# Low parts of weight tiles: an accumulating DMA instead of a VectorE difference

## The chip, the cores and the metric

The kernel runs on 1 core of one Trainium2 chip. The metric is the device time of one execution in microseconds (us). The kernel before takes 1283.22 us, the median of 3 runs (1282.95 to 1283.3). About 0.2% is what a measurement of it can tell from no change.

## The reference

One encoder block for 512 tokens of width 1024, in float32. Two half feed-forwards stand around a token mixer:

```python
x = x + 0.5 * swiglu_ffn(rms_norm(x, ffn1_norm[l]), ffn1_w_gate[l], ffn1_w_up[l], ffn1_w_down[l])
h = rms_norm(x, mix_norm[l])
proj = h @ w_in[l] + b_in[l]
u_a, v_a, q_r, k_r, v_r, g_r, gate_a, gate_b = jnp.split(proj, split_at, axis=-1)
a = spatial_gating(gelu(u_a), gelu(v_a), ...)                    # 128-token chunks
r = bidirectional_retention(rotary(q), rotary(k) / 16, v, ...)   # 4 heads of 256
r = normalised(r) * silu(g_r)
mix = sigmoid(gate_a) * (a @ w_branch_a[l]) + sigmoid(gate_b) * (r @ w_branch_b[l])
x = x + mix @ w_out[l]
x = x + 0.5 * swiglu_ffn(rms_norm(x, ffn2_norm[l]), ffn2_w_gate[l], ffn2_w_up[l], ffn2_w_down[l])
return rms_norm(x, final_norm)
```

`swiglu_ffn(h)` is `(silu(h @ w_gate) * (h @ w_up)) @ w_down` with 2816 hidden units. Nearly all the work is the matrix products with the weights.

## The kernel before

A product in float32 is made of three TensorE passes. Each operand is split into a high part, the value rounded to the type `float32r`, and a low part, the value minus the high part. `mm3` (L90 to L93) adds high times high (L91), the activations' low times the weights' high (L92), and the activations' high times the weights' low (L93; in the token-major products the operands of L92 and L93 change places).

The weights come in tiles. `load_w` (L79) makes one: SP loads the raw tile from HBM by one DMA (L82), ScalarE casts it to the high part (L85), VectorE subtracts (L87). Raw, high and low tiles come from a pool `wp` with 2 buffers each; a buffer is free when its last reader is done. A tile is 128 x 2048 elements, 1,024 KB: 8 rows of blocks of 128 along K and 256 columns of the weight, in pieces of 1 KB in HBM (or 4 rows and 512 columns in the token-major products). TensorE does 48 matmuls with a tile.

There are 106 such tiles. The first feed-forward has 10 pairs of a gate and an up tile (`ag`, `au`; a first pair is loaded in pieces, apart) and 12 down tiles (`ad`, the last four of 768 KB). The mixer has 24 (`q`, `k`, `pv`, `g`, `pva`, `u`), the merge 16 (`ga`, `gb`, `wa`, `wb`), the output projection 4 (`wo`), the second feed-forward 11 pairs (`bg`, `bu`) and 8 down tiles (`bd`). Its last down chunk is split tile by tile elsewhere (`last_weights`).

In `ffn`, `gate_up` uses a pair of tiles in turns: for each half j of the columns first the gate tile, then the up tile. So the order on TensorE is gate j=0, up j=0, gate j=1, up j=1, and then the next pair. Down tiles and the mixer's tiles are used whole, one after the other. `down(0)` stands behind pair 4, `down(1)` behind pair 8.

The norm's factor is applied behind the products: `norm.stats` puts sums on TensorE behind the first gate half, a `pow` on Pool (L132) gives the inverse root, and `spread` brings it to all partitions by a product on TensorE. The loads of the first up tile of a feed-forward and of the first `k` tile are put behind the last square of the norm's sum (`norm.behind`).

The order on each engine is set by a scheduler at build time, from the program order and from the buffers that come free; each engine then runs its instructions in that order. Only the beginning (`first`, the first pair in whole tiles) and the end (`last`) are in written order. Pool does nearly nothing: some memsets, one iota and the `pow`s.

Of the kernel before, what the change touches and what calls it, by code (L numbers as in the profile page):

```python
# [9 lines left out]
F32 = mybir.dt.float32  # L10
# [5 lines left out]
P = 128  # L16
# [13 lines left out]
OFF_U, OFF_V, OFF_Q, OFF_K, OFF_VR, OFF_G, OFF_GA, OFF_GB = (i * 1024 for i in range(8))  # L30
# columns of the per-feature vectors
C_G1, C_GM, C_G2, C_GF, C_B = 0, 8, 16, 24, 32
C_N = 96
# row vectors, broadcast over the partitions
R_BV, R_BVR, R_SG, R_SB, R_BS, R_DEC = 0, 1024, 2048, 3072, 4096, 4608
# [4 lines left out]
def block_kernel(ctx, tc, xT, wg1, wu1, wd1, w_in, wa, wb, wo, wg2, wu2, wd2, cols_d, rows_d, ws_d, cos_d, sin_d, out):  # L40
    nc = tc.nc
    act = ctx.enter_context(tc.tile_pool(name="act", bufs=60))
    wp = ctx.enter_context(tc.tile_pool(name="wp", bufs=2))
    sc = ctx.enter_context(tc.tile_pool(name="sc", bufs=6))
    sm = ctx.enter_context(tc.tile_pool(name="sm", bufs=2))
# [12 lines left out]

# [1 line left out]
    cols = const.tile([P, C_N], F32, name="cols")  # L60
# [11 lines left out]
    def split(src, name, lo_pool=None):  # L72
        """The two parts of a float32 tile that one TensorE pass carries exactly."""
        hi = A(name + "_hi")
        nc.scalar.copy(hi, src)
        lo = A(name + "_lo") if lo_pool is None else lo_pool.tile([P, S], F32R, tag="lo", name=name + "_lo")
        nc.vector.tensor_tensor(out=lo, in0=src, in1=hi.bitcast(F32), op=ALU.subtract)
        return hi, lo

    def load_w(w, k0, nk, c0, nc_, name):  # L80
        raw = wp.tile([P, nk, nc_], F32, tag="raw", name=name + "_raw")
        nc.sync.dma_start(  # L82
            out=raw, in_=w[k0 * P:(k0 + nk) * P, c0:c0 + nc_].rearrange("(k p) c -> p k c", p=P))
        hi = wp.tile([P, nk, nc_], F32R, tag="whi", name=name + "_whi")
        nc.scalar.copy(hi, raw)  # L85
        lo = wp.tile([P, nk, nc_], F32R, tag="wlo", name=name + "_wlo")
        nc.vector.tensor_tensor(out=lo, in0=raw, in1=hi.bitcast(F32), op=ALU.subtract)  # L87
        return hi, lo
# [6 lines left out]
    def proj(o, wt, j, acts, first=True, last=True):  # L95
        """o[feature, token] += w[:, j-th 128 columns].T @ acts"""
        whi, wlo = wt
        n = len(acts)
        for k, (hi, lo) in enumerate(acts):
            mm3(o, whi[:, k, j * P:(j + 1) * P], wlo[:, k, j * P:(j + 1) * P], hi, lo,  # L100
                first and k == 0, last and k == n - 1)

    class Norm:
        """Sum of squares of feature-major tiles, and from it the inverse root mean square."""

# [10 lines left out]
        def behind(self):  # L116
            """Order what follows behind the last term of the sum."""
            stack = ExitStack()
            for ins in self.ins:
                stack.enter_context(tc.issue_after(ins))  # L120
            return stack

        def stats(self, n):
            """Per token, with tokens on the partitions; then on a diagonal, to be spread by `spread`."""
            pt = PS(self.name + "_pss")
# [21 lines left out]
        def spread(self):  # L147
            """The same along the free axis, on all partitions."""
            pb = PS(self.name + "_pbc")
            nc.tensor.matmul(pb, ones_r, self.diag[0], start=True, stop=False)  # L150
            nc.tensor.matmul(pb, ones_r, self.diag[1], start=False, stop=True)
            return pb
# [6 lines left out]
    def scaled_split(x, col, name):  # L159
        """Both parts of x * cols[:, col]."""  # L160
        g = cols[:, col:col + 1]
        hi = A(name + "_hi")
        nc.scalar.activation(hi, x, AF.Copy, scale=g)
        lo = A(name + "_lo")
        nc.vector.scalar_tensor_tensor(out=lo, in0=x, scalar=g, in1=hi.bitcast(F32), op0=ALU.mult, op1=ALU.subtract)
        return hi, lo

    started = []

# [1 line left out]
    def ffn(tag, x, h, norm, wg, wu, wd, on_x, first=None, last=None, last_weights=None, aside=None):  # L171
        """x += 0.5 * swiglu(h); h lacks the factor 1 / rms, which norm gives."""
        bc = None
# [81 lines left out]

# [1 line left out]
    x = [A(f"x{k}", F32) for k in range(KT)]  # L257
    h = []
    norm = Norm("n1")

    def first(pss):
        """The first weights come in pieces along K, so that TensorE can start on the first ones."""
        warm = T("warm")
# [36 lines left out]
    def tables():  # L300
        """Rotary and decay tables of the heads, and the biases of their values."""
        with tc.issue_after(started[0]), tc.issue_after(started[1]), tc.issue_after(started[2]):
# [5 lines left out]

            # log_sigmoid(z) = min(z, 0) - log1p(exp(-|z|)), log1p(e) = 2 atanh(e / (2 + e))
            lg = hp.tile([P, 8], F32, name="lg")  # L310
# [16 lines left out]

            # decay of query t and key s by u = t - (s - p): E[p, u + 384]
            dd = wp.tile([P, 2, EW], F32, tag="raw", name="dd")
# [12 lines left out]

# [1 line left out]
    def bias(col):  # L344
        return cols[:, C_B + col // P:C_B + col // P + 1]

    def tok_proj(o, wt, j0, nk, j, k0, first, last):
        """o[token, column] += h2.T @ w for one tile of tokens"""
        whi, wlo = wt
        for i in range(nk):  # L350
            k = k0 + i
            hi, lo = h2[k][0][:, j * P:(j + 1) * P], h2[k][1][:, j * P:(j + 1) * P]
            mm3(o, hi, lo, whi[:, i, :], wlo[:, i, :], first and i == 0, last and i == nk - 1)

    def tok_block(col, name, between=None):
        """Projection of 512 columns with tokens on the partitions."""
        pv = [PS(name) for _ in range(NT)]
        for half in range(2):
            wt = load_w(w_in, 4 * half, 4, col, 512, f"{name}{half}")
            for j in range(NT):  # L360
                tok_proj(pv[j], wt, 0, 4, j, 4 * half, half == 0, half == 1)
            if half == 0 and between is not None:
                between()
        return pv
# [122 lines left out]

# [1 line left out]
    with ExitStack() as sctx:  # L489
# [86 lines left out]

# [1 line left out]
    mix = []  # L578
# [43 lines left out]

# [1 line left out]
    lp = ctx.enter_context(tc.tile_pool(name="lp", bufs=6))  # L624
# [12 lines left out]
    def last(w, acts):  # L637
        """The last part of the down projection, the final norm and the output, by halves of the tokens,
        so that the first half's norm runs behind the second half's products."""
        nf = len(acts)  # L640
# [75 lines left out]
def _tables():  # L716
    """Rotary angles: they depend on the shapes alone."""
    d = 256
# [38 lines left out]
```

## Time and profile before

| | |
|---|---|
| median of 3 runs | 1283.22 us |
| profiled execution, span | 1281.6 us |
| TensorE busy | 1270.8 us (99%) |
| VectorE busy | 653.1 us (51%) |
| ScalarE busy | 393.6 us (31%) |
| Pool busy | 12.1 us (1%) |
| DMA, share of 16 engines | 30.9%, 126.94 MB |

The profiled execution's span runs from its first to its last instruction; the time of a run is 1.6 us more in the median. An engine's busy time is the sum of its instructions. Matmuls overlap, so a matmul's duration (0.39 us) is longer than the distance to the next (0.227 us); the distance is what counts. The chain that ended last tells which engine sets the end, and the waits of that engine tell what it lacked.

### The profile page before, as it was taken

To read this page: it belongs to the slowest core of one execution; us is meant where nothing else is said; L and a number is where in the kernel's file an instruction comes from. 1 tells how busy PE (TensorE), PEld (TensorE's weight loads), DVE (VectorE), ACT (ScalarE), POOL (GpSimd) and SP (SyncE) were. 2 spreads that over 40 slices of the span, in tenths; PEclk is the share of its full clock that TensorE was granted. 3 is DMA by queue.
4 is the path that set the end of the run, shared out by engine and by line. 5 is a ranking of instruction groups with operands and counts; after the bars stand their busy time and mean duration, and the time that the engine had idled before them with its cause. 6 is when DMAs were issued, how large, how long until landed. Compare 5 with 4: busy or idle time off the path is not lost.

```text
span 1281.6 us, 13501 instructions
## 1 busy us (share of the span) xinstructions
PE 1270.8 (99%) x5787; PEld 1056.0 (82%) x5787; DVE 653.1 (51%) x789; ACT 393.6 (31%) x427; POOL 12.1 (1%) x17
## 2 busy tenths in 40 slices
PE   9999999999999999999999999999999999999997
PEld 6888888888888888888888888888888888888897
DVE  6644355534467575675297434345544434353453
ACT  6322124212243232333244222223322212231232
POOL 0000000000000000000000000000000000000000
PEclk9999999999999999999999999999999999999998
DMA  8223313322343223234223333343242322233221
GB/s 283 80 66 131 98 58 108 111 91 87 113 158 99 66 66 99 67 99 131 66 66 99 99 99 99 99 152 112 66 131 66 129 90 91 86 102 96 90 75 66
DMA packets 116155, 127.79 MB, mean 100 GB/s; under 512 B 2944, under 2 KB 106368, under 8 KB 116096
## 3 DMA queue, kind: packets, MB, share of 16 engines
q1 hardware_dynamic: 116096, 126.94, 30.9%
q8 instruction: 45, 0.74, 0.2%
q14 instruction: 14, 0.11, 0.0%
HBM read 122.74 MB, written 4.19 MB: 99 GB/s over the span
## 4 chain that ended last, share of the span: by engine, by line
PE 99%; DMA 0%; DVE 0%; SPq 0%; ACT 0%; POOLq 0%; issue 0%; DVEq 0%; ACTq 0%
PE apg L91 3%; PE bpd L91 3%; PE bpd L93 3%; PE bpd L92 3%; PE apg L92 3%; PE apg L93 3%; PE apu L91 3%; PE apu L92 3%; PE apu L93 3%; PE bpu L91 3%; PE bpu L93 3%; PE bpg L93 3%; PE apd L92 3%; PE bpg L92 3%; PE apd L91 3%; PE bpu L92 3%
## 5 line engine op out<-in xcount | busy, mean ns | idle before, releaser
L91 PE MATMUL bpu<-h_hi,bu_whi 128*128 128x512 f32 x176 | 68.6, 390 | 0.0
L93 PE MATMUL bpu<-h_hi,bu_wlo 128*128 128x512 f32 x176 | 68.5, 389 | 0.0
L93 PE MATMUL bpg<-h_hi,bg_wlo 128*128 128x512 f32 x176 | 68.5, 389 | 0.0
L92 PE MATMUL bpg<-h_lo,bg_whi 128*128 128x512 f32 x176 | 68.5, 389 | 0.0
L91 PE MATMUL bpg<-h_hi,bg_whi 128*128 128x512 f32 x176 | 68.5, 389 | 0.0
L92 PE MATMUL bpu<-h_lo,bu_whi 128*128 128x512 f32 x176 | 68.5, 389 | 0.0
L91 PE MATMUL apd<-ahid_hi,ad_whi 128*128 128x512 f32 x176 | 68.5, 389 | 0.0
L92 PE MATMUL apd<-ahid_lo,ad_whi 128*128 128x512 f32 x176 | 68.5, 389 | 0.0
L93 PE MATMUL apd<-ahid_hi,ad_wlo 128*128 128x512 f32 x176 | 68.5, 389 | 0.0
L91 PE MATMUL apu<-h_hi,au_whi 128*128 128x512 f32 x160 | 62.4, 390 | 0.0
L93 PE MATMUL apu<-h_hi,au_wlo 128*128 128x512 f32 x160 | 62.3, 389 | 0.0
L93 PE MATMUL apg<-h_hi,ag_wlo 128*128 128x512 f32 x160 | 62.3, 389 | 0.0
L92 PE MATMUL apg<-h_lo,ag_whi 128*128 128x512 f32 x160 | 62.3, 389 | 0.0
L91 PE MATMUL apg<-h_hi,ag_whi 128*128 128x512 f32 x160 | 62.2, 389 | 0.0
L92 PE MATMUL apu<-h_lo,au_whi 128*128 128x512 f32 x160 | 62.2, 389 | 0.0
L91 PE MATMUL bpd<-bhid_hi,bd_whi 128*128 128x512 f32 x128 | 49.8, 389 | 0.0
L92 PE MATMUL bpd<-bhid_lo,bd_whi 128*128 128x512 f32 x128 | 49.8, 389 | 0.0
L93 PE MATMUL bpd<-bhid_hi,bd_wlo 128*128 128x512 f32 x128 | 49.8, 389 | 0.0
L222 DVE SCALAR_TENSOR_TENSOR x<-apd,x 128x512 f32<-128x512 f32 x24 | 16.6, 692 | 58.0 <-PE apd L93 58.0
L203 DVE TENSOR_TENSOR btu<-bpu,n_bc 128x512 f32<-128x512 f32 x22 | 15.2, 691 | 59.0 <-PE bpu L93 59.0
L203 DVE TENSOR_TENSOR atu<-apu,n_bc 128x512 f32<-128x512 f32 x22 | 15.2, 689 | 49.2 <-PE apu L93 49.2
L92 PEld LDWEIGHTS bpu<-h_lo,bu_whi 128*128 128x128 f32 x176 | 33.1, 188 | 6.9
(302 smaller groups left out, 3141.2 us busy)
## 6 DMA issues: line engine op xcount, KB each, us to landing
bg_raw<-in_wg SPq DMA_DIRECT2D x11, 1024.0 KB, 5.3
bu_raw<-in_wu SPq DMA_DIRECT2D x11, 1024.0 KB, 5.3
ag_raw<-in_wg SPq DMA_DIRECT2D x10, 1024.0 KB, 5.3
au_raw<-in_wu SPq DMA_DIRECT2D x10, 1024.0 KB, 5.5
ad_raw<-in_wd SPq DMA_DIRECT2D x8, 1024.0 KB, 5.1
bd_raw<-in_wd SPq DMA_DIRECT2D x8, 1024.0 KB, 5.0
q_raw<-in_w_in SPq DMA_DIRECT2D x4, 1024.0 KB, 5.4
k_raw<-in_w_in SPq DMA_DIRECT2D x4, 1024.0 KB, 5.3
```

Of the source, the lines that this page charges most:

```text
L91: nc.tensor.matmul(o, lhi, rhi, start=first, stop=False)
L92: nc.tensor.matmul(o, lhi, rlo, start=False, stop=False)
L93: nc.tensor.matmul(o, llo, rhi, start=False, stop=last)
L203: nc.vector.tensor_tensor(out=tut, in0=pu, in1=bc, op=ALU.mult)
L222: nc.vector.scalar_tensor_tensor(out=x[m], in0=pd[j], scalar=0.5, in1=x[m], op0=ALU.mult, op1=ALU.add)
```

## The change

The raw load and the cast stay. The low part is now made in two steps: ScalarE writes the raw tile times -1 into the low tile, whose type `float32r` rounds it, so that it holds minus the high part; then a DMA from Pool's queue reads the raw weights once more from HBM and adds them onto the tile. VectorE has no part in it. The raw tile's last reader is now on ScalarE. The low tiles get a pool of their own, `wl`, with 3 buffers instead of 2, and the pool of activation tiles gives up 3 of its 60 buffers for it. Comments and doc strings are dropped, which changes only line numbers.

```diff
-    act = ctx.enter_context(tc.tile_pool(name="act", bufs=60))
+    act = ctx.enter_context(tc.tile_pool(name="act", bufs=57))
     wp = ctx.enter_context(tc.tile_pool(name="wp", bufs=2))
+    wl = ctx.enter_context(tc.tile_pool(name="wl", bufs=3))
...
         hi = wp.tile([P, nk, nc_], F32R, tag="whi", name=name + "_whi")
         nc.scalar.copy(hi, raw)
-        lo = wp.tile([P, nk, nc_], F32R, tag="wlo", name=name + "_wlo")
-        nc.vector.tensor_tensor(out=lo, in0=raw, in1=hi.bitcast(F32), op=ALU.subtract)
+        lo = wl.tile([P, nk, nc_], F32R, tag="wlo", name=name + "_wlo")
+        nc.scalar.activation(lo, raw, AF.Copy, scale=-1.0)
+        nc.gpsimd.dma_start(out=lo, in_=w[k0 * P:(k0 + nk) * P, c0:c0 + nc_].rearrange("(k p) c -> p k c", p=P),
+                            accum_op=ALU.add)
         return hi, lo
```

The order of ScalarE's instructions between pairs 3 and 4 of the first feed-forward. `whi` is a cast, `wlo` a negated copy, `atg` a Silu of a gate half, `ahid_hi` the cast of a hidden unit. Before:

```order
L201 ACTIVATE atg_761<-atg_761 128x512
L75 CAST ahid_hi_767<-atu_764 128x512
L85 CAST ag4_whi_783<-ag4_raw_781 128x2048
L201 ACTIVATE atg_771<-atg_771 128x512
L85 CAST au4_whi_789<-au4_raw_787 128x2048
L75 CAST ahid_hi_777<-atu_774 128x512
```

The same stretch in the changed kernel:

```order
L88 ACTIVATE ag4_wlo_794<-ag4_raw_790 128x2048
L204 ACTIVATE atg_770<-atg_770 128x512
L76 CAST ahid_hi_776<-atu_773 128x512
L86 CAST ag4_whi_792<-ag4_raw_790 128x2048
L204 ACTIVATE atg_780<-atg_780 128x512
L88 ACTIVATE au4_wlo_801<-au4_raw_797 128x2048
L86 CAST au4_whi_799<-au4_raw_797 128x2048
```

The negated copy of the gate tile stands nearly a pair ahead of its cast; that of the up tile comes behind the cast of the gate tile and a Silu, and just ahead of its own cast.

The order on Pool around pairs 3 and 4 in the changed kernel; before there is nothing here but the `pow` (L132, now L135):

```order
L89 DMA ag2_wlo_526<-in_wg1 128x8x256
L135 TENSOR_TENSOR n1_tok_391<-n1_var_389,neghalf_88 128x4
L89 DMA au2_wlo_533<-in_wu1 128x8x256
L89 DMA ag3_wlo_660<-in_wg1 128x8x256
L89 DMA au3_wlo_667<-in_wu1 128x8x256
L89 DMA ag4_wlo_794<-in_wg1 128x8x256
L89 DMA au4_wlo_801<-in_wu1 128x8x256
```

Each accumulating DMA waits in this queue for its negated copy, and what stands behind it waits too.

ScalarE at the start of the second feed-forward, before, with the last square of the norm (`n3_sq`) and the first up tile:

```order
L163 ACTIVATE h3_hi_6046<-xb7_5764,cols_75 128x512
L111 ACTIVATE n3_sq_6050<-xb7_5764 128x512
L85 CAST bu0_whi_6064<-bu0_raw_6062 128x2048
L156 COPY n3_bc_6135<-n3_pbc_6136 128x512
L201 ACT_TABLE_LOAD
```

The same stretch in the changed kernel:

```order
L166 ACTIVATE h3_hi_6125<-xb7_5839,cols_78 128x512
L114 ACTIVATE n3_sq_6129<-xb7_5839 128x512
L86 CAST bu0_whi_6144<-bu0_raw_6142 128x2048
L88 ACTIVATE bu0_wlo_6146<-bu0_raw_6142 128x2048
L88 ACTIVATE bg1_wlo_6295<-bg1_raw_6291 128x2048
L159 COPY n3_bc_6216<-n3_pbc_6217 128x512
```

The cast still comes behind the last square, and the negated copy behind the cast. On TensorE at the same place the changed kernel has the product that spreads the norm (`n3_pbc`) ahead of the first use of `bu0_wlo`:

```order
L131 MATMUL n3_pss_6174<-ones_79,n3_sq_6129 128x2 x4
L94 MATMUL bpu_6191<-h3_hi_5874,bu0_whi_6144 128x512
L95 MATMUL bpu_6191<-h3_lo_5876,bu0_whi_6144 128x512
L153 MATMUL n3_pbc_6217<-n3_diag_hi_6187,ones_r_81 128x512
L154 MATMUL n3_pbc_6217<-n3_diag_lo_6189,ones_r_81 128x512
L96 MATMUL bpu_6191<-h3_hi_5874,bu0_wlo_6146 128x512
```

Before, that product stands behind the whole up half. The low part is still wanted by the third matmul of the up tile. Elsewhere on TensorE only the order within the scores of two heads differs.

## Rows read from the trace of the kernel before

**Rows 1.** The page: busy time by engine, and the chain that ended last.
```profile
span 1281.6 us, 13501 instructions
...
PE 1270.8 (99%) x5787; PEld 1056.0 (82%) x5787; DVE 653.1 (51%) x789; ACT 393.6 (31%) x427; POOL 12.1 (1%) x17
...
PE 99%; DMA 0%; DVE 0%; SPq 0%; ACT 0%; POOLq 0%; issue 0%; DVEq 0%; ACTq 0%
```
**Rows 2.** Waits of TensorE, all: us in total, times, longest.
```profile
PE n_pbc L693 <- DVE n_diag L687: 1.5, 1, 1.5
PE warm L269 <- DVE warm L264: 1.3, 1, 1.3
PE apg L91 <- ACT first_hi L75: 1.1, 1, 1.1
PE n_pss L680 <- ACT n_sq L667: 0.7, 1, 0.7
```
**Rows 3.** Groups by line and form: busy us, mean ns of one; idle before.
```profile
L85 ACT CAST bu_whi<-bu_raw 128x2048 fp32r<-128x2048 f32 x11 | 21.1, 1915 | 41.9 <-issue 24.0 <-PE bpd L92 17.9
...
L75 ACT CAST ahid_hi<-atu 128x512 fp32r<-128x512 f32 x22 | 13.5, 620 | 45.9 <-DVE atu L204 45.9
L163 ACT ACTIVATE h_hi<-x,cols 128x512 fp32r<-128x512 f32 x16 | 11.6, 725 | 20.8 <-DVE x L222 18.1 <-DMA cols<-in_cols 1.7 <-DMA x<-in_xT 0.8
...
L87 DVE TENSOR_TENSOR bu_wlo<-bu_raw,bu_whi 128x2048 fp32r<-128x2048 f32 x11 | 25.2, 2292 | 5.3 <-ACT bu_whi L85 5.3
```
**Rows 4.** The DMA view: one queue, then issues, KB each, median us to landing.
```profile
q1 hardware_dynamic: 116096, 126.94, 30.9%
...
bg_raw<-in_wg SPq DMA_DIRECT2D x11, 1024.0 KB, 5.3
...
ad_raw<-in_wd SPq DMA_DIRECT2D x8, 1024.0 KB, 5.1
...
ad_raw<-in_wd SPq DMA_DIRECT2D x4, 768.0 KB, 4.4
```
**Rows 5.** Timeline between pairs 3 and 4, ScalarE, then TensorE: start us, us.
```profile
91.67 1.91 ACT L85 CAST ag_whi<-ag_raw 128x2048 fp32r<-128x2048 f32 x1 [3.11 <-PE apg L92]
93.49 0.62 ACT L201 ACTIVATE atg<-atg 128x512 f32<-128x512 f32 x1
...
102.76 0.39 PE L92 MATMUL apu<-h_lo,au_whi 128*128 128x512 f32 x1
102.98 0.39 PE L93 MATMUL apu<-h_hi,au_wlo 128*128 128x512 f32 x1
```
**Rows 6.** Timeline between pairs 1 and 2, ScalarE and TensorE.
```profile
50.98 1.13 ACT L75 CAST ahid_hi<-atu 128x512 fp32r<-128x512 f32 x2
...
59.47 0.39 PE L93 MATMUL apu<-h_hi,au_wlo 128*128 128x512 f32 x1
```
**Rows 7.** Timeline of the start, ScalarE and TensorE.
```profile
21.32 1.91 ACT L85 CAST ag_whi<-ag_raw 128x2048 fp32r<-128x2048 f32 x1 [3.13 <-DMA ag_raw<-in_wg]
...
30.78 0.39 PE L93 MATMUL apg<-h_hi,ag_wlo 128*128 128x512 f32 x1
```
**Rows 8.** Timeline at head 0's key tile, ScalarE and TensorE.
```profile
371.17 1.90 ACT L85 CAST k_whi<-k_raw 128x2048 fp32r<-128x2048 f32 x1
...
381.88 0.40 PE L93 MATMUL k<-h_hi,k_wlo 128*128 128x512 f32 x1
```
**Rows 9.** Timeline at the second feed-forward's first up tile, ScalarE and TensorE.
```profile
908.69 1.89 ACT L85 CAST bu_whi<-bu_raw 128x2048 fp32r<-128x2048 f32 x1
...
913.42 0.40 PE L93 MATMUL bpu<-h_hi,bu_wlo 128*128 128x512 f32 x1
```
**Rows 10.** The end by stretches (PEclk after POOL busy), timelines of end and start.
```profile
1273.00:1282.00 9.00, 1.22 (x2) 0.50 (x2) 2.91 (x5) 0.00 (x0) 0.69 (x1) 0.53 0.34 117
...
1270.49 0.28 PE L680 MATMUL n_pss<-ones,n_acc 128*128 128x2 f32 x2
...
10.08 0.63 PE L93 MATMUL apg<-h_hi,first_lo 128*128 128x512 f32 x1
10.51 0.45 PE L91 MATMUL apu<-h_hi,first_hi 128*128 128x512 f32 x1
```

## The prediction

> **What bounds the kernel now.** I read the page's totals and the chain of work that ended last, then who waited for whom on TensorE, then the timeline around the places where a weight tile is first used. TensorE is busy 1270.8 us of the 1281.6 us span, and the chain is 99% TensorE [rows 1]. Its only waits are four, 1.5, 1.3, 1.1 and 0.7 us, and none is for a low part of a weight tile [rows 2]. So there is nothing behind the VectorE difference to win: VectorE is busy 653.1 us, half the span [rows 1], and a VectorE that does less moves no end. The question is only whether the new way delivers each low part before TensorE wants it. The profiled span is 1281.6 us; the median of the runs is 1283.2 us, so I add 1.6 us to a span.
>
> **What is removed.** 106 differences on VectorE (32 tiles in the first feed-forward, 24 in the mixer, 20 in the merge and the output projection, 30 in the second feed-forward), 102 of 2.29 us [rows 3]: some 240 us of work that lies beside TensorE. Gain on the path: 0. I exclude a gain, since no TensorE wait stands behind these instructions.
>
> **What is added on ScalarE.** 106 negated copies of a raw tile, same shape as the cast, 1.91 us [rows 3]. A scaled 128x512 takes 725 ns where a cast of that shape takes 620 [rows 3], so 2.3 us is the upper bound if the scale costs per element; it is a constant here, so I take 1.91. That is 106 x 1.91 = 202 us more on an engine busy 393.6 of 1281.6 us [rows 1]; it fits. What counts is where a copy stands in ScalarE's order (below).
>
> **What is added on the DMA queues.** 106 accumulating transfers on Pool's queue, of 1,024 KB (four of 768). None is in the trace. A plain load of 1,024 KB lands 5.3 us after its issue; 768 KB land in 4.4 us and 1,024 KB in 5.1 us for the same tensor [rows 4]. By these two, 256 KB cost 0.7 us, so a load is 2.3 us fixed and 2.8 us of data. An accumulating one reads the weights, reads what lies in the tile, and writes. Let X be the time from the end of the negated copy to the landing. Lower bound: a plain load, 5.3 us; I exclude less, because the same bytes come from HBM in the same 1 KB pieces. Upper bound: three passes in turn, 3 x 5.3 = 15.9 us, which leaves room for Pool's own part in the issue. I take 2.3 + 2 x 2.8 = 7.9 us for two reads, plus 2.8 us because SP starts the next raw load while it runs: X = 10.7 us.
>
> By the Trainium skill ("DMA: Bandwidth & Descriptors", Anatomy of one DMA — SWDGE (gpsimd) path) a Pool transfer takes 2.0 us plus its bytes at 436 GB/s: 4.4 us for this tile, as an estimate. The plain load from SP took 5.3 us here, longer than that, and no row shows a Pool transfer; with 4.4 us the sum below would be 3.5 us and the time 1286.7 us. The same skill ("Collectives: The Full Stack", The bandwidth ceiling) says that a reducing transfer has half the rate of a copy, for its two source reads. That speaks for doubling the data term, and against the change.
>
> **DMA capacity.** The 106 tiles are 107,520 KB = 110.1 MB of the 126.94 MB that take 30.9% of the DMA engines [rows 4], so 26.8% is theirs. At twice the cost the new transfers need 53.6%, in all 84.5%: it fits. At 2.6 times the sum reaches 100%.
>
> **How long each place can wait.** The low tiles now rotate through three buffers, so a copy can start when the tile three back is used up. Where tiles are used one after the other (down projections, mixer, merge), one tile of 48 matmuls lasts 10.9 us (0.22 to 0.23 us apart, [rows 5], 0.227 in the mean), and two lie between: over 18 us for X, hidden. It is different in the gate/up pairs, because a pair uses its two tiles in turns: gate, up, gate, up, 5.4 us each. The up tile of pair p+1 takes the buffer of the gate tile of pair p, which is free only after its second turn. In ScalarE's new order the high cast of the next gate tile and a Silu stand first, then the negated copy. In the trace that cast starts at 91.67 us and the Silu ends at 94.11 [rows 5], so the copy would end at 96.0. TensorE wants that low part at 102.98 [rows 5]: **room 7.0 us**, stall X - 7.0 = 3.7 us. This holds for pairs 3, 4, 6, 7, 8, 10 of the first and 1, 2, 3, 4, 6, 7, 8, 10 of the second feed-forward, where the pair follows a pair: 14 x 3.7 = **51.8 us**. A stall moves the next release by as much, so it comes again at each pair.
> - Pair 2 of the first feed-forward: two more hidden-unit casts stand before the copy. They end at 52.1 us [rows 6], the copy at 54.0, the low part is wanted at 59.47 [rows 6]: room 5.5, stall **5.2 us**.
> - The start: the first gate cast ends at 23.2 us [rows 7], the copy at 25.1, the wish is at 30.78 [rows 7]: room 5.7, stall **5.0 us**. The up tile's cast and copy follow until 28.9; its wish comes 24 matmuls after the gate tile's, past 36.2, so its room is 7.3 us plus the first stall, and it adds nothing.
> - Key tile of head 0, which is held back behind the norm's last square: cast from 371.17 us, copy until 375.0, wanted at 381.88 [rows 8]: room 6.9, stall **3.8 us**.
> - The first up tile of the second feed-forward, held back in the same way: cast from 908.69 us, copy until 912.5, wanted at 913.42 [rows 9]: room 0.9, stall **9.8 us**. Before, the 2.29 us difference ended just in time. This place stalls by 4.4 us even at the plain load's X. The norm's `pow` stands behind this transfer on Pool; TensorE needs it only 2 matmuls into the tile, and what it loses there lies inside the same stall, as long as the issue takes Pool under 9 us.
>
> Three activation buffers fewer, and a wo load that now stands ahead of one of the reloaded x tiles on SP: the x tile is wanted only after its first output projection, so I price both at 0; if that cover were gone it would be at most a full plain load, 5.3 us [rows 4].
>
> **Sum.** 51.8 + 5.2 + 5.0 + 3.8 + 9.8 = 75.6 us; 1281.6 + 75.6 + 1.6 = **1358.8 us**. At X = 5.3 only 913.42 stalls: 4.4 us, 1287.6 us. At X = 15.9: 14 x 8.9 + 10.4 + 10.2 + 9.0 + 15.0 = 169.2 us, 1452.4 us.
>
> **Rivals.**
> - *A fast transfer* (X from 3.5 to 7.0). The pairs hide it; left are 913.42 and little else: 1286 to 1296 us. For it: plain loads land in 5.3 us, and the engines are two thirds idle. Against: a second read, and Pool must make the issue. The Trainium skill's fit (above) would put the time here.
> - *The transfer becomes the bound* (X over 13.5, or more than 2.6 times a plain load on the engines). At three times, 30.9 + 3 x 26.8 = 111% of the span: 1426 us by capacity, 1452 us by latency, more if one issue keeps Pool for over 10.9 us a tile. For it: no row shows what the addition or Pool's issue costs.
> - *The clock falls in the stalls.* At the end TensorE does only 128x2 matmuls from 1270.49 us, waits 1.5 us [rows 2], and the granted clock of the last 9 us is 0.53, which is the 1.2 GHz level [rows 10]. At the start matmuls stand 0.43 us apart until 10.51 us and then at full pace [rows 10]. If every one of 18 stalls cost some 10 matmuls at 0.2 us more, that is 36 us: 1395 us.
> - *Not slower.* It decides at one place, 913.42: with X at 3.5 us or less the stall there is 2.6 us or less and all others are gone, so the time is at most 1285.8 us. It needs an accumulation that lands before a plain load would. Against: even 768 KB take 4.4 us plain [rows 4].
>
> **How the numbers follow.** Forecast (X 7 to 13.5, 1297 to 1410 us) 0.45; fast transfer 0.18; bound by transfers 0.22; clock 0.12; not slower 0.03. The range runs from the lower to the upper bound of X, 1288 to 1452 us, and leaves out the last case, the lowest part of the fast one and half of the bound one. About 0.2%, 2.6 us, is what a measurement can tell from no change: faster 0.01 and same 0.02 (the two together are the last case), slower 0.97.
>
> **What would show it.** In the profile after: waits of TensorE for the low tiles, by a DMA from Pool; about 3.7 us at each of 14 pairs, about 10 us at the first up tile of the second feed-forward, none in the down projections and the merge; the accumulating transfers landing some 10 us after their issue; VectorE near 410 us, ScalarE near 595; DMA share near 80%. Waits in the down projections too would mean the engines or Pool are the bound. If the pairs show no wait, X is under 7. A granted clock under 1.0 between pairs would show the clock rival. The prediction is wrong if ScalarE's copies start later than their place says, for then the rooms are shorter than I read them.

## Result and profile after

The changed kernel takes 1394.92 us (median; 1394.79 to 1395.37), the kernel before 1283.2 us (1282.95 to 1283.3): ratio 1.0874, 95% interval 1.0858 to 1.0889. It is slower by 112 us, where 75.6 us were forecast. In the fences below line numbers are three higher than in the rows of before (a high cast is L86, the negated copy L88, Pool's transfer L89, the three products L94 to L96).

The page of the changed kernel, first its span, then busy time by engine (us, share of the span, instructions) and the DMA queues (q0 is Pool's, q1 SP's: packets, MB, share of 16 engines):

```profile
span 1393.6 us, 13794 instructions
...
PE 1303.9 (94%) x5787; PEld 1074.3 (77%) x5787; DVE 421.9 (30%) x683; ACT 582.6 (42%) x535; POOL 175.5 (13%) x123
...
q0 software_dynamic: 105120, 110.11, 50.6%
q1 hardware_dynamic: 116096, 126.94, 28.3%
```

Against [rows 1]: VectorE gave up 231 us and nothing came of it; TensorE's share fell from 99% to 94%. Two things happened to TensorE. It **waits** 89.7 us (1393.6 - 1303.9) where it waited 10.8 (1281.6 - 1270.8): 78.9 us more. And its **busy time grew** by 33.1 us (1303.9 against 1270.8) for the same 5787 matmuls. Together 112.0 us, which is all of the difference of the spans.

The waits of TensorE in the changed kernel (us in total, times, longest), to be held against the four of [rows 2]:

```profile
PE bpu L96 <- DMA bu_wlo<-in_wu: 32.3, 9, 5.7
PE apu L96 <- DMA au_wlo<-in_wu: 26.9, 7, 6.1
PE apg L96 <- DMA ag_wlo<-in_wg: 8.8, 1, 8.8
PE k L96 <- DMA k_wlo<-in_w_in: 4.4, 1, 4.4
PE n_pbc L153 <- DVE n_diag_hi L143: 2.8, 1, 2.8
PE nr_pbc L153 <- DVE nr_diag_hi L143: 2.4, 1, 2.4
```

The four large ones are for a low part, by a DMA, at gate/up pairs, the start and the key tile of head 0; the last two, at products that spread a norm, come below. One pair in the timeline (start us, us), ScalarE, Pool, then TensorE; it answers to [rows 5]:

```profile
87.29 1.91 ACT L86 CAST ag_whi<-ag_raw 128x2048 fp32r<-128x2048 f32 x1 [3.12 <-PE apg L95]
89.11 0.63 ACT L204 ACTIVATE atg<-atg 128x512 f32<-128x512 f32 x1
89.63 1.90 ACT L88 ACTIVATE au_wlo<-au_raw 128x2048 fp32r<-128x2048 f32 x1
...
91.83 1.55 POOL L89 DMA_DIRECT2D au_wlo<-in_wu  x1 [22.08 <-ACT au_wlo L88]
...
101.64 0.50 PE L96 MATMUL apu<-h_hi,au_wlo 128*128 128x512 f32 x1 [2.88 <-DMA au_wlo<-in_wu]
```

Cast, Silu and negated copy stand in ScalarE's order as the forecast had them. The copy ends at 91.53 us, the low part is wanted at 98.76 (101.64 less the 2.88 of waiting) and is there at 101.64: the room, from the copy's end to the wish, is 7.2 us, and the time to the landing 10.1 us. Pool is free for 22 us before, so no queue on Pool holds this transfer up.

The extra busy time stands behind the waits. TensorE after another one, that of pair 2:

```profile
73.82 0.80 PE L96 MATMUL apu<-h_hi,au_wlo 128*128 128x512 f32 x1 [4.75 <-DMA au_wlo<-in_wu]
74.41 0.63 PE L94 MATMUL apu<-h_hi,au_whi 128*128 128x512 f32 x1
74.83 0.63 PE L95 MATMUL apu<-h_lo,au_whi 128*128 128x512 f32 x1
...
80.21 0.39 PE L96 MATMUL apu<-h_hi,au_wlo 128*128 128x512 f32 x1
80.44 0.39 PE L94 MATMUL apu<-h_hi,au_whi 128*128 128x512 f32 x1
```

For 6 us the matmuls start 0.43 us apart, then 0.23 again. The same by stretches (us, busy time of PE, PEld, DVE, ACT and POOL, then the granted clock, DMA share, GB/s):

```profile
74.00:80.00 6.00, 6.00 (x15) 4.70 (x16) 0.00 (x0) 0.00 (x0) 0.00 (x0) 0.50 1.18 204
...
480.00:560.00 80.00, 80.00 (x358) 66.27 (x358) 42.81 (x69) 37.57 (x38) 10.13 (x7) 1.00 0.78 166
720.00:960.00 240.00, 240.00 (x1093) 200.01 (x1092) 73.30 (x112) 111.99 (x94) 33.66 (x22) 1.00 0.94 198
```

The granted clock is 0.50, the 1.2 GHz level, behind the wait (the DMA share of so short a stretch is rough). In a stretch of the mixer (480 to 560 us) and from the mixer's end through the merge into the output projection (720 to 960 us) TensorE never waits, at a DMA share up to 0.94, and its clock stays at 1.00.

### The profile page after: what moved, and what is told of

Same layout as the page of the kernel before. It is cut to its first block, busy times and chain, and to the rows that moved or that the text cites. A ratio compares the mean times of both kernels' runs of the same rounds, so it can differ in the third digit from the quotient of the medians.

```text
span 1393.6 us, 13794 instructions
## 1 busy us (share of the span) xinstructions
PE 1303.9 (94%) x5787; PEld 1074.3 (77%) x5787; DVE 421.9 (30%) x683; ACT 582.6 (42%) x535; POOL 175.5 (13%) x123
## 3 DMA queue, kind: packets, MB, share of 16 engines
q0 software_dynamic: 105120, 110.11, 50.6%
## 4 chain that ended last, share of the span: by engine, by line
PE 47%; issue 36%; DMA 8%; POOL 5%; ACT 3%; DVE 1%; SPq 0%; POOLq 0%; DVEq 0%; ACTq 0%
DMA u_raw<-in_w_in 2%; DMA bu_wlo<-in_wu 2%; PE pgt L94 2%; PE pgt L96 2%; PE pgt L95 2%; PE bpd L94 2%; PE bpd L95 2%; PE bpd L96 2%; PE k L96 1%; PE k L94 1%; PE k L95 1%; PE po L96 1%; PE pb L96 1%; PE pb L94 1%; PE pa L96 1%
## 5 line engine op out<-in xcount | busy, mean ns | idle before, releaser
L96 PE MATMUL bpu<-h_hi,bu_wlo 128*128 128x512 f32 x176 | 75.2, 427 | 32.3 <-DMA bu_wlo<-in_wu 32.3
L96 PE MATMUL apu<-h_hi,au_wlo 128*128 128x512 f32 x160 | 68.1, 426 | 26.9 <-DMA au_wlo<-in_wu 26.9
L94 PE MATMUL bpu<-h_hi,bu_whi 128*128 128x512 f32 x176 | 73.3, 417 | 0.0
L95 PE MATMUL bpu<-h_lo,bu_whi 128*128 128x512 f32 x176 | 73.3, 416 | 0.0
L96 PE MATMUL apg<-h_hi,ag_wlo 128*128 128x512 f32 x160 | 63.4, 396 | 8.8 <-DMA ag_wlo<-in_wg 8.8
L96 PEld LDWEIGHTS bpu<-h_hi,bu_wlo 128*128 128x128 f32 x176 | 36.1, 205 | 44.0 <-DMA bu_wlo<-in_wu 36.2
L94 PE MATMUL apd<-ahid_hi,ad_whi 128*128 128x512 f32 x176 | 68.5, 389 | 0.0
L96 PE MATMUL apd<-ahid_hi,ad_wlo 128*128 128x512 f32 x176 | 68.5, 389 | 0.0
L94 PE MATMUL bpg<-h_hi,bg_whi 128*128 128x512 f32 x176 | 68.5, 389 | 0.0
L96 PE MATMUL bpg<-h_hi,bg_wlo 128*128 128x512 f32 x176 | 68.5, 389 | 0.0
L94 PE MATMUL apu<-h_hi,au_whi 128*128 128x512 f32 x160 | 67.0, 419 | 0.0
L95 PE MATMUL apu<-h_lo,au_whi 128*128 128x512 f32 x160 | 66.7, 417 | 0.0
L94 PE MATMUL apg<-h_hi,ag_whi 128*128 128x512 f32 x160 | 63.0, 394 | 0.0
L96 PEld LDWEIGHTS apu<-h_hi,au_wlo 128*128 128x128 f32 x160 | 32.9, 205 | 37.0 <-DMA au_wlo<-in_wu 29.9
L76 ACT CAST bhid_hi<-btu 128x512 fp32r<-128x512 f32 x22 | 13.6, 617 | 101.9 <-DVE btu L207 101.9
L94 PE MATMUL bpd<-bhid_hi,bd_whi 128*128 128x512 f32 x128 | 49.8, 389 | 0.0
## 6 DMA issues: line engine op xcount, KB each, us to landing
bg_wlo<-in_wg POOLq DMA_DIRECT2D x11, 1024.0 KB, 11.8
```

Source lines behind the costliest of these rows:

```text
L94: nc.tensor.matmul(o, lhi, rhi, start=first, stop=False)
L95: nc.tensor.matmul(o, lhi, rlo, start=False, stop=False)
L96: nc.tensor.matmul(o, llo, rhi, start=False, stop=last)
```

## Experiments

Theory: a transfer of some 10 us starts only when a buffer comes free, 7 us ahead of the wish, and each wait also lets the clock fall. Rivals: the DMA engines or their contention are the bound; the smaller activation pool costs the time; Pool's part or the number of pieces, not the addition, makes the transfer long. Every ratio is set against runs of the kernel before on the same chip, 1281.7 to 1281.9 us there. Differences in us against the changed kernel are between chips, and can be off by the 1.3 us or so by which the kernel before differs (1283.2 us in the section above).

**Pools alone.** The kernel before with

```
-    act = ctx.enter_context(tc.tile_pool(name="act", bufs=60))
+    act = ctx.enter_context(tc.tile_pool(name="act", bufs=57))
+    wl = ctx.enter_context(tc.tile_pool(name="wl", bufs=3))
...
-        lo = wp.tile([P, nk, nc_], F32R, tag="wlo", name=name + "_wlo")
+        lo = wl.tile([P, nk, nc_], F32R, tag="wlo", name=name + "_wlo")
```

> The kernel before with the changed kernel's pools alone (three low buffers, 57 activation buffers), VectorE difference kept. Latency theory: TensorE stays 99% busy, 1283 us (1281 to 1286). Rival, the smaller activation pool or the other order of instructions costs part of the 112 us: over 1290.

1281.94 us, ratio 0.9997 (0.9988 to 1.0006). The pools and the order of instructions that comes with them cost nothing; the rival of the smaller pool is out.

**The transfer without the addition.** In the changed kernel:

```
-        nc.gpsimd.dma_start(out=lo, in_=w[...].rearrange("(k p) c -> p k c", p=P),
-                            accum_op=ALU.add)
+        nc.gpsimd.dma_start(out=lo, in_=w[...].rearrange("(k p) c -> p k c", p=P))
```

> The same Pool transfer from HBM without the addition (the low part then holds the raw weight: the subtraction is left out); order and buffers as in the changed kernel. If the second read makes the transfer long: landing 7 to 8 us after issue in place of 10 to 12, waits at the pairs under 1 us, left about 5 us at the start and 5 us at the first up tile: 1300 us (1290 to 1320). If Pool's part or the 1 KB pieces make it long: landing stays near 10 us and the time at 1385 to 1395.

1299.13 us, ratio 1.0138 (1.0112 to 1.0164). The low part is then the raw weight, so the numbers computed are others; only the time counts. The page's rows of Pool's queue and of one tile's transfers (KB each, median us to landing):

```profile
q0 software_dynamic: 105120, 110.11, 37.6%
...
bu_wlo<-in_wu POOLq DMA_DIRECT2D x11, 1024.0 KB, 6.0
```

Pool's own time for these issues, from the view of the tile (ns, min/median/max, then first and last start):

```profile
L89 POOL DMA_DIRECT2D bu_wlo<-in_wu x11: 873/873/882, 919.8 to 1227.7; - x11
```

The same two in the changed kernel, the page's row and the tile's:

```profile
bu_wlo<-in_wu POOLq DMA_DIRECT2D x11, 1024.0 KB, 9.9
```

```profile
L89 POOL DMA_DIRECT2D bu_wlo<-in_wu x11: 1549/1549/1559, 973.8 to 1318.6; - x11
```

Same order of instructions on every engine, same bytes, same pieces; the accumulation alone costs some 96 us. It lengthens the landing from 6.0 to 9.9 us; Pool's issue, 0.68 us longer, explains little of that. (The median landings of the tiles of 1,024 KB in this kernel run from 5.8 to 7.4 us.) On the DMA engines the transfers take 50.6% of 1393.6 = 705 us with it and 37.6% of 1297.5 = 488 us without; the plain loads of the same tiles, 26.8% of 1281.6 by the forecast's working, are 343 us.

**Another order in a pair.** In the changed kernel, `gate_up`:

```
-            for j in range(2):
-                pg = PS(f"{tag}pg"); proj(pg, wt[0], j, h)
-                pu = PS(f"{tag}pu"); proj(pu, wt[1], j, h)
+            for j in range(2): ... proj(pgs[j], wt[0], j, h)
+            for j in range(2): ... proj(pus[j], wt[1], j, h)
```

> A pair does both gate halves, then both up halves. The gate tile's buffer is then free at the middle of the pair and the next up tile is wanted 21.8 us after that. Latency theory: the pair waits go, the first up tile of the second feed-forward is wanted 5.4 us later (wait 8.6 down to about 3), start 8.8 and key tile 4.4 stay: 1270.8 + 30 idle + 8 clock + 1.6 = 1310 us (1302 to 1322). Rival, DMA capacity or contention: waits move to other tiles, 1370 to 1395.

1309.98 us, ratio 1.0212 (1.0194 to 1.0231): 85 us less, with every transfer kept. Its largest waits on TensorE:

```profile
PE apg L96 <- DMA ag_wlo<-in_wg: 7.1, 1, 7.1
PE bpu L96 <- DMA bu_wlo<-in_wu: 4.9, 1, 4.9
PE k L96 <- DMA k_wlo<-in_w_in: 4.1, 1, 4.1
```

No pair after a pair waits; of the waits for a low part those at the start, the first up tile of the second feed-forward and the key tile are left. The up tiles' transfers land after 9.0 us (10.0 and 9.9 in the changed kernel), still longer than a room of 7.2: it is the longer room that hides them, and the DMA engines carry the same bytes in a shorter span.

The same order in the kernel before is the control:

> The kernel before with gate, gate, up, up in a pair, VectorE difference kept: the control for that order. If the order by itself gains or costs nothing: 1281 to 1284 us. If it helps by itself (below 1278), the gain of 85 us in the changed kernel is not the room alone.

1282.26 us, ratio 1.0005 (0.9996 to 1.0014). The order gains nothing by itself.

**Only tiles used one after the other.** In the changed kernel the gate and up tiles and the first key tile get the VectorE difference back:

```
+        if not acc:
+            nc.vector.tensor_tensor(out=lo, in0=raw, in1=hi.bitcast(F32), op=ALU.subtract)
+            return hi, lo
```

> Accumulating transfers only for tiles that are used one after the other (down projections, mixer, merge, output projection: 61 of 106); VectorE difference for the gate/up pairs and the first key tile. Latency theory: no low tile is waited for; what stays are two places in the mixer where the power instruction stands behind a transfer's issue on Pool (2.4 and 1.1 us): 1286 us (1282 to 1290). Rival, contention of these transfers with the raw loads costs by itself: over 1295.

1287.58 us, ratio 1.0042 (1.003 to 1.0055), with 63 accumulating transfers (the expectation's 61 is a miscount). That is 5.8 us more than the kernel before, so they are not quite free. Of the waits for a low part one is left, 0.7 us at a query tile; the largest new wait is another:

```profile
PE nr_pbc L156 <- DVE nr_diag_hi L146: 2.3, 1, 2.3
```

So 62 of 63 transfers of some 9 to 12 us are hidden where a tile has over 18 us. The wait at the norm does not come from Pool's queue, as the expectation has it: `v_hi`, which the norm needs, stands on ScalarE behind a negated copy that waits 5.4 us (more in the section on the prediction).

**The waits filled with work.** In the changed kernel, at the 15 pairs that wait:

```
+                if j == 0 and p in fill:
+                    for _ in range(15):
+                        nc.tensor.matmul(pu, wt[0][0][:, KT - 1, 0:P], h[KT - 1][0], start=True, stop=True)
                 proj(pu, wt[1], j, h)
```

> The changed kernel with 15 extra matmuls (3.4 us at 0.227 us each, their result overwritten) ahead of the up tile at the 15 gate/up pairs that wait for 2.9 to 6.1 us, so that TensorE works where it waited. If the idle time lets the clock fall: TensorE works at full pace behind these places, its clock at 0.5 is left at the start, the key tile and the first up tile, and the time falls by 20 to 28 us to 1370 us (1362 to 1378). If the slow stretches come from elsewhere (the load of the DMA queues, the power of the work): the extra matmuls only fill time, 1394 to 1400.

1378.52 us, ratio 1.0753 (1.0738 to 1.0768): 225 matmuls more and 16.4 us less, against the 20 to 28 expected. Busy time on the page of this kernel:

```profile
PE 1336.2 (97%) x6012; PEld 1105.6 (80%) x6012; DVE 421.4 (31%) x683; ACT 582.2 (42%) x535; POOL 175.6 (13%) x123
```

Its largest waits:

```profile
PE apg L97 <- DMA ag_wlo<-in_wg: 6.7, 1, 6.7
PE apu L97 <- DMA au_wlo<-in_wu: 6.1, 5, 3.5
PE bpu L97 <- DMA bu_wlo<-in_wu: 5.4, 1, 5.4
```

Less 225 x 0.227 = 51.1 us TensorE is busy 1285.1 us, 18.8 us less than in the changed kernel; idle and filler together are 39.9 + 51.1 = 91.0 us, as good as the 89.7 before. So the time that came back is the clock's, and the idle time was its cause. The second feed-forward behind its first pair shows it, by stretches as above, in the changed kernel and then here:

```profile
990.00:1340.00 350.00, 323.37 (x1369) 263.89 (x1368) 75.39 (x111) 132.54 (x108) 41.92 (x27) 0.97 0.78 168
990.00:1340.00 350.00, 350.00 (x1588) 291.28 (x1587) 79.02 (x119) 136.08 (x117) 41.91 (x27) 1.00 0.78 168
```

The granted clock is 1.00 throughout at the same DMA share of 0.78. The gain is smaller than expected: in the first feed-forward five up tiles still waited 6.1 us in sum, the longest 3.5 us with a slow stretch behind it, and where the wait was 2.9 us the filler of 3.4 was too long.

**Two halves.**

```
+        for i0, i1 in ((0, nk // 2), (nk // 2, nk)):
+            nc.gpsimd.dma_start(out=lo[:, i0:i1, :], in_=w[(k0 + i0) * P:(k0 + i1) * P, ...]..., accum_op=ALU.add)
```

> Each accumulating transfer in two, four K tiles each. The first product waits for the first half alone, the second half is wanted 2.7 us later. Latency theory: the pair waits of 2.9 to 3.5 us shrink by up to 2.7 us, start, key tile and first up tile by as much; with the clock that then falls less: 1330 us (1315 to 1350). Rival, Pool's issue has a fixed cost for each transfer, or both halves run side by side and land together: waits as before, 1390 to 1410.

1332.11 us, ratio 1.0389 (1.0375 to 1.0403). Of the 14 pairs twelve wait 0.6 to 1.6 us, one 2.1 and the one at 233 us 3.1. The waits for the second feed-forward's up tiles, 32.3 us in the changed kernel, are here:

```profile
PE bpu L99 <- DMA bu_wlo<-in_wu: 16.6, 9, 7.8
```

The price is on Pool: both issues of a tile take 2.6 us together, where one took 1.55 (the timeline, start us, us).

```profile
1012.77 2.61 POOL L90 DMA_DIRECT2D bu_wlo<-in_wu  x2 [14.85 <-ACT bu_wlo L88]
```

**The copy on VectorE.**

```
-        nc.scalar.activation(lo, raw, AF.Copy, scale=-1.0)
+        nc.vector.tensor_scalar(out=lo, in0=raw, scalar1=-1.0, scalar2=None, op0=ALU.mult)
```

> The negated copy on VectorE in place of ScalarE, else the changed kernel. If the copy's place behind a cast and a Silu on ScalarE shortens the room: the copy ends 1.5 to 2.5 us earlier, pair waits of 3.1 fall to 1 to 1.5 us, the clock falls less: 1345 us (1325 to 1365). If ScalarE's order costs nothing (the transfer's end is set by the engines): 1385 to 1395.

1347.71 us, ratio 1.0507 (1.0491 to 1.0523). A negated copy takes 1.22 us there and no longer stands behind a cast and a Silu; TensorE waits 59.8 us (1351.0 - 1291.2) in place of 89.7. Thirteen of the 14 pairs still wait 0.6 to 3.4 us, most 2.0 to 2.7. That is less relief than expected; the up tiles' transfers now take 11.1 and 10.8 us, where they took 9.9 and 10.0.

**A fourth low buffer.** The simplest mend, and it failed:

```
-    act = ctx.enter_context(tc.tile_pool(name="act", bufs=57))
-    wl = ctx.enter_context(tc.tile_pool(name="wl", bufs=3))
+    act = ctx.enter_context(tc.tile_pool(name="act", bufs=53))
+    wl = ctx.enter_context(tc.tile_pool(name="wl", bufs=4))
```

> Fourth buffer for low tiles (four activation buffers fewer), else the changed kernel. Latency theory (a transfer of about 11 us starts only when a buffer comes free, 7 us before the wish): the 14 waits at the gate/up pairs go, 53.5 us of the 89.7 us idle; left are the start 8.8, the key tile 4.4, the first up tile of the second feed-forward 8.6 and small ones, with 8 to 10 us of slow clock behind them: 1317 us (1308 to 1327). Rival, the DMA engines or contention are the bound: the same bytes move, so 1380 to 1395. Rival, fewer activation buffers cost the time: no faster than 1394.9.

1470.39 us, ratio 1.1466 (1.1439 to 1.1493), slower than all others. The waits for low parts at the pairs are gone (1.7 and 0.2 us are left), and new ones have come, 74 us of them for high parts:

```profile
PE pgt L94 <- ACT gb_whi L86: 15.2, 4, 4.6
PE pb L94 <- ACT wb_whi L86: 14.5, 3, 5.6
...
PE apu L96 <- DMA au_wlo<-in_wu: 1.7, 1, 1.7
```

Where they come from shows in the merge, ScalarE, then SP:

```profile
820.06 1.88 ACT L86 CAST ga_whi<-ga_raw 128x2048 fp32r<-128x2048 f32 x1
833.76 1.91 ACT L88 ACTIVATE wa_wlo<-wa_raw 128x2048 fp32r<-128x2048 f32 x1 [11.81 <-DMA wa_raw<-in_wa]
...
836.09 1.89 ACT L86 CAST gb_whi<-gb_raw 128x2048 fp32r<-128x2048 f32 x1
...
821.97 0.37 SPq L83 DMA_DIRECT2D wa_raw<-in_wa  x1
838.00 0.37 SPq L83 DMA_DIRECT2D wb_raw<-in_wb  x1
```

With a buffer always free the scheduler put the copy of the next tile (`wa_wlo`) ahead of the cast of this one (`gb_whi`). There are two raw buffers; `wa_raw` can be loaded only when `ga_whi` is cast (821.97), and lands some 11.7 us later, issued 1.5 us behind an accumulating transfer. Only then can the copy `wa_wlo` run, and behind it the cast `gb_whi`, which frees the buffer for `wb_raw`. Cast, load and copy have become one ring of 16 us (821.97 to 838.00) around 10.9 us of matmuls.

To hold that apart from the smaller pool and from the fourth buffer itself, the same kernel with ScalarE's order kept:

```
-        nc.scalar.activation(lo, raw, AF.Copy, scale=-1.0)
+        with tc.issue_after(casts[-1]) if len(casts) > 1 else ExitStack():
+            nc.scalar.activation(lo, raw, AF.Copy, scale=-1.0)
+        casts.append(cast)
```

> Four low buffers and 53 activation buffers as in the run with four buffers (1470 us), but a negated copy may not stand ahead of the cast of the tile before it on ScalarE, so that ScalarE's order is nearly that of the changed kernel. If that run's new waits came from ScalarE's order (a cast behind a copy that waits for the raw load after next): they go, the pair waits of about 3 us come back, since a copy stands behind a cast that waits for the same buffer release, and the time is 1385 to 1398 us. If they came from the smaller activation pool or from the fourth buffer's traffic: it stays above 1440.

1385.11 us, ratio 1.0804 (1.0787 to 1.0822). The ring is gone, so the order made it, and the pair waits are back: 31.4 us for the second feed-forward's up tiles, 25.4 for the first's. A fourth buffer gives little (1385 against 1395 us) as long as the copy stands behind a cast that waits for a release itself.

**The source on the chip.**

```
-        nc.gpsimd.dma_start(out=lo, in_=w[...].rearrange("(k p) c -> p k c", p=P), accum_op=ALU.add)
+        nc.gpsimd.dma_start(out=lo, in_=raw, accum_op=ALU.add)
```

> The accumulating transfer takes the raw weights from the raw tile on the chip in place of HBM: 8 KB in a row for each partition in place of eight pieces of 1 KB. If the number of pieces makes the landing long: Pool's issue far under 1.55 us, landing 6 to 8 us, pair waits under 1.5 us; but the raw buffer is held until the landing, so raw loads start later; 1310 to 1350 us. If the addition is bound by its bytes: landing 9 to 11 us as before and, with the raw loads held, 1395 to 1480.

1318.69 us, ratio 1.0285 (1.027 to 1.03). Landing on the page of this kernel, and Pool's issue in the view of the tile:

```profile
bu_wlo<-bu_raw POOLq DMA_DIRECT2D x11, 1024.0 KB, 7.3
```

```profile
L89 POOL DMA_DIRECT2D bu_wlo<-bu_raw x11: 859/869/872, 933.0 to 1245.7; - x11
```

The same addition of the same bytes in 7.3 us, and 0.87 us on Pool; TensorE waits at most 2.9 us for a low part, and for no high part of a weight tile, so holding the raw buffer longer made no new wait there. So the addition's price is not by its bytes alone; whether the source (HBM or the chip) or the size of the pieces makes it, this run changes both and leaves open.

**All mends together**: gate, gate, up, up; the copy on VectorE; two halves.

> All three mends together, every weight tile still accumulated: gate, gate, up, up; the negated copy on VectorE; each transfer in two halves. By the latency theory the start wait falls from 7.1 to about 2.5 us, the key tile's from 4.1 to 0, the first up tile's from 4.9 to about 2, no pair waits: idle 17 to 20 us, 1293 us (1286 to 1300). Below 1283 cannot be, since TensorE's 1271 us of work stay.

1289.68 us, ratio 1.0061 (1.0046 to 1.0075), with all 106 tiles accumulated. Busy time on its page, then the largest wait:

```profile
PE 1271.7 (99%) x5787; PEld 1055.9 (82%) x5787; DVE 534.9 (42%) x789; ACT 398.2 (31%) x429; POOL 288.7 (22%) x229
```

```profile
PE apg L99 <- DMA ag_wlo<-in_wg: 3.4, 1, 3.4
```

TensorE's busy time is that of before to 0.9 us: with one long wait left the clock costs next to nothing. It is still 8 us over the kernel before; nothing here beats that, since nothing takes work from TensorE.

## Why the prediction was right, and where its size was off

- **The bound: right.** No wait for VectorE, no gain. VectorE went from 653.1 to 421.9 us and the pools alone changed nothing.
- **ScalarE's copies: right.** 1.91 us each were taken, and 1.91 measured; ScalarE came to 582.6 us against near 595.
- **X: right as a sum.** 10.7 us were taken as fixed cost, two reads and some sharing; the pair above shows 10.1, and the median landings at the gate and up tiles are 9.9 to 11.8 us. No run measures the three parts one by one. In time of the DMA engines the factor of two holds against SP's plain loads: 705 against 343 us, 2.05. The Trainium skill ("Collectives: The Full Stack", The bandwidth ceiling) gives the reducing transfers of a collective half the rate of its copies; against a copy in Pool's own queue this case shows 705 to 488, 1.45. Its fit for a Pool transfer ("DMA: Bandwidth & Descriptors", Anatomy of one DMA — SWDGE (gpsimd) path), 4.4 us as an estimate for this tile, does not hold here: a plain copy from Pool landed in 5.8 us at the shortest median, an accumulating one at a gate or up tile in 9.9; the measurements decide, and with them the rival of the fast transfer falls.
- **DMA capacity: right.** 84.5% forecast, 78.9% in the two queues. That the engines are not the bound is shown by the merge (0.94 share without a wait) and by the order in a pair, which gave 85 us back at the same bytes. The rival of the bound by transfers falls.
- **The rooms: right in sum.** At the 14 pairs 48.8 us (2.9 to 4.1 us, one of 6.1) against 51.8; pair 2 4.75 against 5.2; the key tile 4.4 against 3.8; the first up tile 5.7 + 2.85 at the norm's product, which now stands two matmuls into it, = 8.6 against 9.8. The start was mis-sized: 8.8 against 5.0, for TensorE came there at 29.1 us where before it came at 30.78 [rows 7], and the copy's end lay 12.7 us ahead of the landing. All these are 75.3 us against 75.6; that they agree so closely is luck, for the misses cancel. The pair of 6.1 us has an activation table load of 1.28 us ahead of its copy on ScalarE, which the forecast's pattern did not see, and 11.9 us from the copy's end to the landing.
- **Missed: ScalarE's order in the mixer.** 2.4 us at a head's norm and 1.1 at the normed scale came on top, 3.5 us. At both places a negated copy stands on ScalarE ahead of work that the norm needs, and waits for a raw load; what stands behind it waits too. ScalarE ahead of the first and the second place, and Pool's power instruction ahead of the first:

```profile
586.10 1.91 ACT L88 ACTIVATE k_wlo<-k_raw 128x2048 fp32r<-128x2048 f32 x1 [5.49 <-DMA k_raw<-in_w_in]
587.91 0.60 ACT L76 CAST v_hi<-vt 128x512 fp32r<-128x512 f32 x1
...
702.20 1.91 ACT L88 ACTIVATE u_wlo<-u_raw 128x2048 fp32r<-128x2048 f32 x1 [11.54 <-DMA u_raw<-in_w_in]
704.02 0.56 ACT L159 COPY nr_bc<-nr_pbc 128x512 f32<-128x512 f32 x1
...
593.60 1.45 POOL L135 TENSOR_TENSOR nr_tok<-nr_var,neghalf 128x4 f32<-128x4 f32 x1 [3.69 <-DVE nr_var L133]
```

Pool was idle for 3.69 us ahead of its power instruction, so no transfer's issue held that up; it waited for VectorE, which had waited 4.58 us for `v_hi`. Pool's queue, which the forecast weighed for the second feed-forward, is not what cost time here. With the copy on VectorE neither wait is there.

- **Mis-sized: the clock, a term of 0 where TensorE's busy time grew by 33.1 us.** The forecast priced the stalls alone and kept the clock as a rival at 0.12, with 36 us and 1395 us. That rival is what came. Behind the waits for low parts the matmuls at 0.43 us apart add 1.6 to 3.0 us each, but for two places with 0.1; by the starts of the matmuls that is some 31 us in all with the small ones. The rest is not the clock's: the last matmul before each new wait has no next one that overlaps it (0.39 against 0.227 us). Filling the waits at the pairs took 18.8 us of the busy time away. The rows for it were there: 0.53 at the end behind a wait, 0.43 us apart at the start [rows 10]. The mistake was to treat it as another case, though it follows from the stalls themselves: it belonged into the sum, 75.6 + 36 us. That this sum gives 1395 us to the digit is luck too, for the waits were 3 us more and the clock 3 us less. And the measured time lies inside the stated range because X was left open from 5.3 to 15.9 us; the range holds no clock at all.

Sum as measured: 75.3 + 3.5 of waits, 33.1 of longer busy time = 111.9 us, of 112.0.

## What to carry to other kernels

Before work is moved from an idle engine to a DMA, set the new latency against the room between the release of its buffer and the wish, place by place: 63 such transfers at tiles used in turn cost 5.8 us in all, and the interleaved order of the pairs alone cost 85 us, so the order of the matmuls was the cheapest mend. To each TensorE wait of some 3 us add what its clock takes afterwards, here in sum some 0.4 of the waits again (some 31 us behind 78.9 of new waits). Look at what stands behind an instruction that waits for a transfer on an engine that works in order: here a norm waited for it. A deeper pool changes what the scheduler puts first: look at the order that comes out of it, for a fourth buffer turned 1395 us into 1470.

## What was not expected of the hardware

- Of two waits of 2.9 us one was followed by 1.67 us of slow matmuls (at 1236.50 us) and one by 0.1 (at 101.64 us); one of 3.02 us (at 1091.81) lost 0.1 as well. The length of a wait alone does not say whether the clock falls. What does was not tried. The 6 us behind the one at 101.64 and the one at 1236.50, the granted clock third from the end:

```profile
102.00:108.00 6.00, 6.00 (x28) 4.96 (x27) 0.93 (x2) 0.00 (x0) 0.00 (x0) 1.00 1.22 226
1237.00:1243.00 6.00, 6.00 (x21) 4.73 (x20) 0.00 (x0) 0.00 (x0) 0.00 (x0) 0.72 1.21 223
```

- Pool's own time for one issue of 1,024 KB depends on what it moves: 1.55 us accumulating from HBM, 0.87 copying the same pieces, 0.87 accumulating from the chip in 8 KB rows, 2.6 for two accumulating halves.
- A raw load can take some 11.7 us, as in the ring above, against 5.3 alone [rows 4]; that was in the forecast's X only as sharing. It goes with when the load is issued: in the changed kernel the 26 raw loads issued 1.5 to 2.8 us behind an accumulating transfer that was still under way landed after 8.9 to 12.8 us, while those issued with none under way had a median of 5.3. In the four-buffer kernel 53 loads were issued within 3 us behind one (8.6 to 14.4 us). Why the load waits so long was not tried.
